# Loading sample rows into idle grid columns, a state update in two rounds, and an output projection spread between attention units

## The chip, the cores and the metric

The kernel runs on one NeuronCore of a Trainium2 chip. The metric is the device time of one execution in microseconds (us); lower is better.

## The reference

One inference step of a streaming encoder with two layers, for 256 frames of a prompt (two blocks of 128 tokens) and 8 streams of 16 frames (a third block, the "sample" block): D = 1024, all in fp32.

```python
for l in range(DEPTH):                        # DEPTH = 2
    xn = rmsnorm(h, norm_mix[l])
    if l == 0: mix = mamba_mixer(xn, ...)     # in-projection, conv of width 4, SSD scan in 8 groups, gate, out-projection
    else:      mix = attention(xn, shared K/V of the stream) @ w_o + b_o   # window 128, sinks, 16 heads, 4 KV heads
    h = h + mix
    h = h + peer(rmsnorm(h, norm_ffn[l]), ...)
y = rmsnorm(h, norm_final)

def peer(xn, w_q, sub_k1, sub_k2, u_tab, v_tab):       # per token: 8 heads, 16 experts of 128*128 each
    q = xn @ w_q;  top 16 of q1 @ sub_k1, of q2 @ sub_k2, then of the 16*16 sums -> eid (128 per token), gate = softmax
    act = gelu(sum_d u_tab[eid] * xn)
    return sum_k (gate * act) * v_tab[eid]
```

## The kernel before

**Layout and precision.** A weight tile of 128x1024 comes as `raw` over SP's queue, ScalarE casts it to `hi` (line 108) and VectorE subtracts to get `lo` (line 109); a product is three matmuls (`hi*hi`, `hi*lo`, `lo*hi`, lines 144 to 146 for `gemm_cols`, line 157 for `gemm_rows`). Matmul results go to one pool of eight PSUM banks (`bank`). The order of each engine's instructions is fixed ahead of the run by a planner that goes through the program with its own estimates of durations; instructions in `pin(...)` keep their program order, the others it may move.

**Scan (`mamba`).** Eight groups of four heads. Each group has conv tiles `b_tile`, `c_tile` and two `x_tile`s (24 matmuls of 384 columns each), then `decay` (line 455: 12 VectorE operations on `ab`, rows fetched over SP), `states`, `outputs`, `turn` (transposes of `y`, line 529) and `carry` (line 542: the new states of the sample streams, eight small matmuls into four banks, added to `s0` by four VectorE operations, line 545), and `store`. A group's later steps run within the next group's tiles; group 1 has an order of its own. The last group's run inside the out-projection of 16 tiles (`out_terms`), whose accumulators hold six banks.

**PEER (`peer`).** The prompt blocks are done densely: `u_step(e2)` for e2 = 0 to 127 multiplies the prompt by a tile of `u` and writes gelu into the grid `G` (`G[0]`: columns 0 to 63, `G[1]`: 64 to 127; a column e of a half is 128x256). In the second half `w_step` multiplies one-hot gate weights into `G[0]` (VectorE's `og`, `oa`, line 1176), and `v_step(e2)` for 128 more steps multiplies the grid by `v`. So a layer has 256 steps s: 0 to 63, 64 to 127 (second half), 128 to 255 (value stage).
The sample block is done by gathering. Its 128 tokens are in four groups of 32, and the block's 128 experts' rows of `u` are gathered in 32 steps per group over POOL's queue (line 1094) into `gath` (three buffers). VectorE multiplies each gathered tile by the group's rows `xg` and sums (line 1132, `u_item`). `xg` is 128x1024, loaded by `load_group` from `xrow` in DRAM over POOL's queue (line 918); it has one buffer, so group g+1 is loaded when item 31 of group g is done. `tick(s)` says how many items are due at step s (`U_DUE`): 30 by step 64, 72 by 128, 110 by 192, 128 by 216. At every 32nd item it pauses for two steps. Rows of `v` for the sample tokens are gathered into idle columns of the grid (`fetch_v`), 24 of them into columns 48 to 63 of `G[1]` before those are written, the rest into `G[0]` when the value stage has read its first columns, and `v_quad` multiplies them.

**Attention.** Sixteen units in the order p p p p s s s s p p p p s s s s (p: a prompt block and a KV head, two banks of scores; s: two sample streams and two KV heads, one bank). In iteration i a unit's mask and scores are made, the transposes of unit i-2 and the values of unit i-3 (`masks`, `transposes`, `scores`, `values`, all pinned). The results are collected in `oT`. Behind the last unit comes the output projection: eight tiles `ct`, three blocks, 144 matmuls of 512 columns in six accumulator banks. Then the norm of `peer(1)`: sums of squares on ScalarE, `rstd` on POOL, `xn` on VectorE (line 896, into `qTp`), transposes (line 905), splits, and the query projection (lines 144 to 146).

Of the kernel before, what the change touches and what calls it, by code (L numbers as in the profile page):

```python
# [9 lines left out]
F32 = mybir.dt.float32  # L10
# [51 lines left out]
def encoder_step(ctx: ExitStack, tc: tile.TileContext, t_in, t_out):  # L62
# [160 lines left out]
    def mamba(h_src):  # L223
        with ExitStack() as c:
# [68 lines left out]
            if True:  # L293
# [103 lines left out]
                class Group:  # L397
# [133 lines left out]

                    def carry(self):

                        s0 = self.s0
                        dve.tensor_tensor(s0.rearrange("p s (r d) -> p s r d", d=64),
                                          s0.rearrange("p s (r d) -> p s r d", d=64),
                                          decS[:, :, self.hs].unsqueeze(3).to_broadcast([P, NSEQ, 4, 64]), op=OP.mult)
                        pss = [bank([P, 2, 256]) for _ in range(4)]
                        for w in range(2):
                            for q in range(4):  # L540
                                rows = slice(32 * q, 32 * q + 32)
                                pin(pe.matmul(pss[q][:, w], self.Bt[rows, 2 + w], self.xde[rows, 2],
                                              start=True, stop=True, tile_position=(32 * q, 0)))
                        for k in range(4):
                            dve.tensor_tensor(s0[:, 2 * k:2 * k + 2], s0[:, 2 * k:2 * k + 2], pss[k], op=OP.add)

# [5 lines left out]
                for g in range(GROUPS):  # L552
                    G_ = Group(g)
                    gs.append(G_)
                    if g == 2:
                        for nm in ("k", "v"):
                            pin(pool.dma_start(t_out["sm_" + nm][:, 0:P - TS, :], t_in["cache_" + nm][:, TS:P, :]))
                    prev = gs[g - 1] if g else None
                    G_.b_tile()
                    if g > 1:  # L560
                        G_.fetch()
                        prev.states()
                        prev.outputs()
                    G_.c_tile()
                    if g == 1:
                        prev.decay()
                        G_.fetch()
                    if g == 0:
                        st_ = steps()
                        next(st_)  # L570
                    if g > 1:
                        prev.turn()
                    G_.x_tile(0)
                    if g == 1:
                        prev.states()
                        prev.outputs()
                        prev.turn()
                    if g:
                        prev.carry()
                    G_.x_tile(1)  # L580
                    if g == 0:
                        G_.gate()
                        next(st_, None)
                        G_.fetch()
                    else:
                        G_.decay()
                        G_.gate()
                        prev.store()
                    G_.tokens()
# [4 lines left out]
                def out_terms():  # L594
                    for ct in range(16):
                        if ct == 2:
                            last.states()
                            last.outputs()
                        elif ct == 5:
                            last.turn()  # L600
                        elif ct == 7:
                            last.carry()
                        elif ct == 9:
                            last.store()
                            sync.dma_start(t_out["convs"], cst)
                        yield (load_split(t_in["w_out"][ct * P:(ct + 1) * P, :]),
                               lambda b, ct=ct: yhi[:, ct, b * P:(b + 1) * P],
                               lambda b, ct=ct: ylo[:, ct, b * P:(b + 1) * P]), 15 - ct
# [14 lines left out]
    def attention():  # L623
        with ExitStack() as c:
# [158 lines left out]
            def transposes(u):  # L783
                PT[u] = []
                for q, sm in enumerate(P_.pop(u)):
                    nkb = sm.shape[2] // P
                    pt = bank([P, 2, nkb, P])
                    for j in range(2):
# [3 lines left out]
                        "p (n k q) -> p n k q", k=nkb, q=P)  # L792
                    if q:
                        dve.tensor_copy(pT, pt)
# [40 lines left out]
            ohi = T(late, [P, 8, NT], F32R, tag="ohi")  # L835
            olo = T(late, [P, 8, NT], F32R, tag="olo")

            def out_terms():
                for ct in range(8):
                    split(ohi[:, ct], olo[:, ct], oT[:, ct])  # L840
                    yield (load_split(t_in["w_o"][ct * P:(ct + 1) * P, :]),
                           lambda b, ct=ct: ohi[:, ct, b * P:(b + 1) * P],
                           lambda b, ct=ct: olo[:, ct, b * P:(b + 1) * P]), 7 - ct

            for i in range(len(todo) + LAG + 1):
                if i in (5, 6, 7):
# [9 lines left out]
                if i in q_at:  # L856
                    q_tile(q_at[i])

            accs = [[bank([P, 512]) for _ in range(2)] for _ in range(NB)]
            gemm_row_loop(accs, out_terms())  # L860
            for b in range(NB):
# [5 lines left out]
    def peer(l):  # L867
        with ExitStack() as c:
# [20 lines left out]
            qTp = T(qpool, [P, 2 * PH, NP], F32, tag="qTp")  # L889
            grow = brow(t_in["ffn_rows"][l], D, qpool, "grow")  # L890
            h = hold["h"]
# [23 lines left out]
            def load_group(g):  # L915
                xg[g] = T(one, [P, D], F32, tag="xg", bufs=1)
                rows = xrow[g]
# [185 lines left out]
            def fetch_v(n, s):  # L1103

                half, e = (1, HE - 16 + 4 * (n % 4)) if s < 2 * HE else (0, 4 * (n % v_bufs(s)))
                assert all(k != (half, e) for k, _ in vrows.values())
# [20 lines left out]
            def u_item(k):  # L1127
# [6 lines left out]
                if j == TG - 1:  # L1134
                    if g + 1 < GR:
                        load_group(g + 1)
                    lay = T(one, [P, GR, TG], F32, tag="cm", bufs=2)
# [81 lines left out]
            done = {"u": 0, "v": 0, "f": 0}  # L1219
            start, paused = [0], {}  # L1220

            def tick(s):
# [6 lines left out]
                want = P if s >= U_DUE[-1][0] else n0 + (n1 - n0) * (s + 1 - s0) // (s1 - s0)  # L1229
                if done["u"] % TG == 0 and done["u"]:  # L1230
                    if s < paused.setdefault(done["u"], s + 2):
                        return
                while done["u"] < want:
# [8 lines left out]
            def quads(s):  # L1242

                while done["v"] < 32 and V_DUE[done["v"]] <= s:
                    v_quad(done["v"])
                    done["v"] += 1
                if s >= 2 * HE - 16 and done["f"] == 4 * V_FIRST and s < 2 * HE + 17:
                    return
# [40 lines left out]
            gpools.append(c.enter_context(tc.tile_pool(name="pg1", bufs=1)))  # L1289
            G[1] = T(gpools[1], [P, HE, NP], F32, tag="G1")  # L1290
            out_s = [bank([P, 512]) for _ in range(2)]
            for e2 in range(HE):
# [11 lines left out]
            for e2 in range(2 * HE):  # L1304
                v_step(e2)
                tick(2 * HE + e2)
                if e2 < HE and e2 % 2 == 1:
# [125 lines left out]
```

## Time and profile before

| | us |
|---|---|
| median of 3 runs | 2586.1 |
| lowest and highest | 2566.3, 2592.02 |
| profiled execution | 2582.15 |
| its span, first to last instruction | 2579.4 |

In the profile PE is TensorE's matmuls, PEld its weight loads (they overlap), DVE VectorE, ACT ScalarE, POOL GpSimd, SP the queue that issues most transfers. Times count from the start of the span. In a timeline row the brackets at the end say how long the engine was idle before the instruction and what ended that. The mean granted clock of TensorE is 0.971 of full speed over the span.

### The profile page before, as it was taken

How to read it: one execution, taken by the hardware profiler on the slowest of the kernel's cores; microseconds unless marked ns; L12 is line 12 of the kernel's file. 1: busy time of each engine (PE TensorE's matmuls, PEld its weight loads, DVE VectorE, ACT ScalarE, POOL GpSimd, SP SyncE). 2: the span in 40 equal slices, each digit the busy share in tenths (PEclk: the TensorE clock that was granted, in tenths of full speed). 3: DMA queues.
4: the chain of work that ended last, by engine and by line, in shares of the span. 5: the costliest groups of instructions: out<-in, count | busy, mean ns of one | idle time of the engine just before them, and what ended most of it. 6: DMA issues, size and time to landing. Idle time of an engine off the chain costs nothing.

```text
span 2579.4 us, 44478 instructions
## 1 busy us (share of the span) xinstructions
PE 2438.5 (95%) x16656; PEld 2046.8 (79%) x16656; DVE 1874.9 (73%) x4151; ACT 1242.6 (48%) x2410; POOL 702.1 (27%) x755
## 2 busy tenths in 40 slices
PE   8899998999989999998999998999989989999998
PEld 7899978999978876666666878999989876656676
DVE  5888736979867797677655645979878788678655
ACT  5555524433546555454344544433456655545343
POOL 2222200022333124346431100012333224346431
PEclk9999998999989999999999979999999999999999
DMA  5445434477879889889996414467789888989995
GB/s 191 171 170 191 155 110 150 149 246 257 287 267 319 254 274 344 299 336 372 362 340 192 131 34 149 139 223 261 281 276 325 268 270 324 322 328 363 371 333 210
DMA packets 179193, 647.67 MB, mean 251 GB/s; under 512 B 23761, under 2 KB 25665, under 8 KB 176321
## 3 DMA queue, kind: packets, MB, share of 16 engines
q1 hardware_dynamic: 99360, 363.76, 40.7%
q0 software_dynamic: 79616, 281.08, 30.9%
q8 instruction: 130, 2.13, 0.3%
q14 instruction: 87, 0.70, 0.1%
HBM read 628.52 MB, written 18.06 MB: 251 GB/s over the span
## 4 chain that ended last, share of the span: by engine, by line
PE 74%; DVE 12%; DMA 8%; issue 2%; ACT 2%; another core or an unknown queue 1%; POOL 0%; SPq 0%; POOLq 0%; DVEq 0%; ACTq 0%
PE bank L157 25%; PE bank L146 10%; PE bank L144 10%; PE bank L145 10%; PE bank L1151 4%; DVE lo L109 3%; PE bank L1160 3%; PE bank L1207 3%; DMA xg<-xrow 2%; DVE gath L1132 2%; PE bank L1193 2%; DMA gath<-in_p_u,eidU 1%; DMA raw<-in_u_t 1%; ACT hi L108 1%; DVE lox L109 1%
## 5 line engine op out<-in xcount | busy, mean ns | idle before, releaser
L108 ACT CAST hi<-raw 128x1024 fp32r<-128x1024 f32 (+1 forms) x475 | 493.6, 1040 | 594.0 <-PE bank L145 362.3
L109 DVE TENSOR_TENSOR lo<-raw,hi 128x1024 fp32r<-128x1024 f32 (+1 forms) x475 | 575.4, 1213 | 214.2 <-ACT hi L108 207.4
L1094 POOL DMA_INDIRECT gath<-in_p_u,eidU x256 | 310.0, 1211 | 948.5 <-DVE gath L1132 515.8
L146 PE MATMUL bank<-xhi,lo 128*128 128x256 f32 (+1 forms) x1344 | 409.9, 306 | 22.8 <-DVE lo L109 22.6
L144 PE MATMUL bank<-xhi,hi 128*128 128x256 f32 (+1 forms) x1344 | 409.1, 305 | 1.2 <-ACT hi L108 1.2
L145 PE MATMUL bank<-xlo,hi 128*128 128x256 f32 (+1 forms) x1344 | 402.3, 299 | 0.0
L1094 POOL DMA_INDIRECT G<-in_p_v,eidT x256 | 281.4, 1099 | 310.3 <-PE bank L1151 231.1
L1132 DVE SCALAR_TENSOR_TENSOR gath<-gath,xg 128x1024 f32<-128x1024 f32 x256 | 310.8, 1217 | 69.9 <-DMA gath<-in_p_u,eidU 40.6
L146 PEld LDWEIGHTS bank<-xhi,lo 128*128 128x128 f32 x1344 | 259.6, 193 | 31.4 <-DVE lo L109 26.9
L144 PEld LDWEIGHTS bank<-xhi,hi 128*128 128x128 f32 x1344 | 260.1, 194 | 12.4 <-ACT hi L108 6.3
L108 ACT CAST phi<-G 128x256 fp32r<-128x256 f32 x232 | 93.2, 404 | 366.5 <-PE bank L157 310.1
L145 PEld LDWEIGHTS bank<-xlo,hi 128*128 128x128 f32 x1344 | 259.9, 193 | 0.3
L144 PE MATMUL bank<-qhi,hi 128*128 128x256 f32 (+1 forms) x792 | 245.4, 310 | 9.8 <-ACT xf L907 8.2
L146 PE MATMUL bank<-qhi,lo 128*128 128x256 f32 (+1 forms) x792 | 239.6, 303 | 2.2 <-DVE lo L109 2.2
L145 PE MATMUL bank<-qlo,hi 128*128 128x256 f32 (+1 forms) x792 | 239.8, 303 | 0.0
L157 PE MATMUL bank<-hi,phi 128*128 128x512 f32 x640 | 202.6, 411 | 13.2 <-ACT phi L108 8.3
L157 PE MATMUL bank<-lo,phi 128*128 128x512 f32 x640 | 204.4, 399 | 7.2 <-DVE lo L109 6.9
L1186 ACT ACTIVATE oa<-ioh,e2T 128x128 f16<-128x128 f16 x512 | 163.1, 390 | 83.7 <-PE bank L1193 61.7
L109 DVE TENSOR_TENSOR plo<-G,phi 128x256 fp32r<-128x256 f32 x232 | 97.5, 422 | 144.7 <-PE bank L157 139.3
L157 PE MATMUL bank<-hi,plo 128*128 128x512 f32 x640 | 201.6, 397 | 0.0
L157 PEld LDWEIGHTS bank<-hi,phi 128*128 128x128 f32 x640 | 117.9, 190 | 69.6 <-ACT hi L108 17.5
L144 PEld LDWEIGHTS bank<-qhi,hi 128*128 128x128 f32 x792 | 152.4, 192 | 11.3 <-ACT xf L907 8.7
(358 smaller groups left out, 4764.7 us busy)
## 6 DMA issues: line engine op xcount, KB each, us to landing
raw<-in_u_t SPq DMA_DIRECT2D x256, 512.0 KB
raw<-in_p_v SPq DMA_DIRECT2D x256, 512.0 KB
raw<-in_w_in SPq DMA_DIRECT2D x32, 512.0 KB
raw<-in_p_w_q SPq DMA_DIRECT2D x32, 512.0 KB
raw<-in_w_z SPq DMA_DIRECT2D x16, 512.0 KB
s<-in_state_ssm SPq DMA_DIRECT2D x8, 1024.0 KB
out_sm_ssm<-s SPq DMA_DIRECT2D x8, 1024.0 KB
raw<-in_w_out SPq DMA_DIRECT2D x16, 512.0 KB
```

The source lines that it names most:

```text
L108: act.copy(hi, raw)
L109: dve.tensor_tensor(lo, raw, hi32, op=OP.subtract)
L144: pe.matmul(ps, whi[:, s], xhi[:, k, c0:c1], start=(k == 0), stop=False)
L145: pe.matmul(ps, whi[:, s], xlo[:, k, c0:c1], start=False, stop=False)
L146: pe.matmul(ps, wlo[:, s], xhi[:, k, c0:c1], start=False, stop=(k == KD - 1))
L157: mm = pe.matmul(ps, x, w[:, hf * n:(hf + 1) * n], start=s_, stop=e_)
L1094: pool.indirect_dma_start(out=tile_, out_offset=None, in_=tab, in_offset=bass.IndirectOffsetOnAxis(ap=idx, axis=0))
L1132: pin(dve.scalar_tensor_tensor(tile_, tile_, 1.0, xg[g], op0=OP.mult, op1=OP.mult, accum_out=au[g][:, j:j + 1]))
L1151: pin(pe.matmul(out_s[hf][32 * q:32 * q + 32, :], cm[:, q], rows[q][:, hf * 512:hf * 512 + 512], start=(r == 0), stop=(r == 31), tile_posi ...
L1160: pe.matmul(ps, raw[:, k * P:(k + 1) * P], xf[:, k], start=(k == 0), stop=(k == KD - 1))
L1186: act.activation(a[:, i], ioh, AF.Square, scale=-1.0, bias=e2T[:, t, 0:1])
L1207: pe.matmul(accs[b][hf], G[e2 // HE][:, e2 % HE, b * P:(b + 1) * P], raw[:, hf * 512:hf * 512 + 512], start=False, stop=False)
```

## The change

In `peer`, odd groups of sample rows get places of their own: group 1 in columns 60 to 63 of `G[1]`, loaded when that half is allocated; group 3 in columns 32 to 35 of `G[0]`, loaded after step 35 of the value stage. Groups 0 and 2 keep `xg`; group 2 is loaded when group 0 ends. The pause goes. The gathered `v` rows of the second half move from columns 48 to 63 to 44 to 59, and the row `grow` of norm weights is put into columns 60 to 63 of `G[0]`.

In the scan, the last group's `carry` runs in two rounds of two banks. In group 1 the previous group's `decay` comes after `x_tile(0)`, its `carry` after `x_tile(1)`, and its `turn` after the group's own `decay`.

In attention, tiles 0 to 3 of the output projection are done for the two prompt blocks between the last four units (four accumulators); the sample block's part of these tiles comes after the units, with the four tiles of `w_o` loaded and split a second time, and then tiles 4 to 7. The copies of the sample units' transposes go to VectorE.

```diff
-                    def carry(self):
+                    def carry(self, n=4):
...
-                        pss = [bank([P, 2, 256]) for _ in range(4)]
-                        for w in range(2):
-                            for q in range(4):
-                                rows = slice(32 * q, 32 * q + 32)
-                                pin(pe.matmul(pss[q][:, w], self.Bt[rows, 2 + w], self.xde[rows, 2],
-                                              start=True, stop=True, tile_position=(32 * q, 0)))
-                        for k in range(4):
-                            dve.tensor_tensor(s0[:, 2 * k:2 * k + 2], s0[:, 2 * k:2 * k + 2], pss[k], op=OP.add)
+                        for q0 in range(0, 4, n):
+                            pss = {q: bank([P, 2, 256]) for q in range(q0, q0 + n)}
+                            for w in range(2):
+                                for q in pss:
+                                    rows = slice(32 * q, 32 * q + 32)
+                                    pin(pe.matmul(pss[q][:, w], self.Bt[rows, 2 + w], self.xde[rows, 2],
+                                                  start=True, stop=True, tile_position=(32 * q, 0)))
+                            for q in pss:
+                                dve.tensor_tensor(s0[:, 2 * q:2 * q + 2], s0[:, 2 * q:2 * q + 2], pss[q], op=OP.add)
...
                     G_.c_tile()
                     if g == 1:
-                        prev.decay()
                         G_.fetch()
...
                     G_.x_tile(0)
                     if g == 1:
+                        prev.decay()
                         prev.states()
                         prev.outputs()
-                        prev.turn()
-                    if g:
+                    if g > 1:
                         prev.carry()
                     G_.x_tile(1)
...
+                        if g == 1:
+                            prev.carry()
                         G_.decay()
+                        if g == 1:
+                            prev.turn()
                         G_.gate()
...
-                            last.carry()
+                            last.carry(2)
...
-                    if q:
+                    if q or u[0] == "s":
                         dve.tensor_copy(pT, pt)
...
+            first = len(todo) - 4
             for i in range(len(todo) + LAG + 1):
...
-            accs = [[bank([P, 512]) for _ in range(2)] for _ in range(NB)]
-            gemm_row_loop(accs, out_terms())
+                if i == first - 1:
+                    accs += [[bank([P, 512]) for _ in range(2)] for _ in range(2)]
+                if 0 <= i - first < 4:
+                    ct = i - first
+                    out_split(ct)
+                    gemm_rows(accs, [out_term(ct)], ct == 0, False)
+
+            accs.append([bank([P, 512]) for _ in range(2)])
+            for ct in range(4, 8):
+                out_split(ct)
+
+            shift = lambda term: (term[0], lambda b: term[1](b + 2), lambda b: term[2](b + 2))
+            for ct in range(4):
+                gemm_rows(accs[2:], [shift(out_term(ct))], ct == 0, False)
+            gemm_rows(accs, [out_term(4)], False, False)
+            gemm_rows(accs, [out_term(5)], False, False)
+            gemm_rows(accs, [out_term(6), out_term(7)], False, True)
...
-            grow = brow(t_in["ffn_rows"][l], D, qpool, "grow")
+
+            grow = G[0][:, HE - 4:].rearrange("p e t -> p (e t)")
+            src = t_in["ffn_rows"][l]
+            sync.dma_start(grow, bass.AP(tensor=src.tensor, offset=src.offset, ap=[[0, P], [1, D]]))
...
             def load_group(g):
-                xg[g] = T(one, [P, D], F32, tag="xg", bufs=1)
+
+                if g % 2:
+                    xg[g] = (G[1][:, HE - 4:] if g == 1 else G[0][:, 32:36]).rearrange("p e t -> p (e t)")
+                else:
+                    xg[g] = T(one, [P, D], F32, tag="xg", bufs=1)
...
-                half, e = (1, HE - 16 + 4 * (n % 4)) if s < 2 * HE else (0, 4 * (n % v_bufs(s)))
+                half, e = (1, HE - 20 + 4 * (n % 4)) if s < 2 * HE else (0, 4 * (n % v_bufs(s)))
...
                 if j == TG - 1:
-                    if g + 1 < GR:
-                        load_group(g + 1)
+                    if g == 0:
+                        load_group(2)
...
-                if done["u"] % TG == 0 and done["u"]:
-                    if s < paused.setdefault(done["u"], s + 2):
-                        return
...
             G[1] = T(gpools[1], [P, HE, NP], F32, tag="G1")
+            load_group(1)
...
                 v_step(e2)
+                if e2 == 35:
+                    load_group(3)
```

## Rows read from the trace of the kernel before

**Rows 1.** The page's engine table: busy us (share of the span) xinstructions.
```profile
PE 2438.5 (95%) x16656; PEld 2046.8 (79%) x16656; DVE 1874.9 (73%) x4151; ACT 1242.6 (48%) x2410; POOL 702.1 (27%) x755
```

**Rows 2.** Waits of the whole span: waiting engine and line <- releaser: us, times, longest.
```profile
DVE gath L1132 <- DMA gath<-in_p_u,eidU: 40.6, 11, 8.6
...
DVE gath L1132 <- DMA xg<-xrow: 29.2, 4, 7.6
```

**Rows 3.** Timeline of VectorE at first items of groups 1 and 3: start, us, instruction.
```profile
715.91 1.23 DVE L1132 SCALAR_TENSOR_TENSOR gath<-gath,xg 128x1024 f32<-128x1024 f32 x1 [7.59 <-DMA xg<-xrow]
...
1089.11 1.23 DVE L1132 SCALAR_TENSOR_TENSOR gath<-gath,xg 128x1024 f32<-128x1024 f32 x1 [8.64 <-DMA gath<-in_p_u,eidU]
```

**Rows 4.** Timeline of TensorE behind the first of these waits.
```profile
719.81 0.58 PE L146 MATMUL bank<-xhi,lo 128*128 128x256 f32 x1 [6.64 <-DVE lo L109]
```

**Rows 5.** Windows: stretch, us, PE PEld DVE ACT POOL busy (xinstructions), PEclk, DMA share, GB/s.
```profile
705.00:755.00 50.00, 40.70 (x346) 38.18 (x344) 31.25 (x50) 22.41 (x47) 12.13 (x11) 0.83 0.75 242
755.00:882.00 127.00, 122.56 (x1199) 112.73 (x1198) 100.22 (x154) 78.26 (x159) 39.33 (x39) 0.99 0.88 301
882.00:923.00 41.00, 35.67 (x331) 34.81 (x330) 30.53 (x48) 23.17 (x48) 8.15 (x8) 0.92 0.79 238
1877.00:1923.00 46.00, 38.40 (x355) 35.56 (x355) 31.57 (x51) 22.64 (x47) 12.15 (x11) 0.89 0.81 264
2050.00:2090.00 40.00, 34.50 (x326) 33.64 (x325) 29.92 (x48) 22.60 (x48) 8.16 (x8) 0.91 0.79 236
```

**Rows 6.** Timeline of POOL: the first gather into the second half's grid.
```profile
689.59 1.01 POOL L1094 DMA_INDIRECT G<-in_p_v,eidT  x1 [1.70 <-ACT xlo L1275]
```

**Rows 7.** Chain that ended last, in time, around boundaries 1, 2 and 3: start, us, what.
```profile
699.80 16.08 DMA xg<-xrow
...
887.49 14.40 DMA xg<-xrow
...
1068.75 0.47 POOL xg L918
...
1069.79 19.20 DMA gath<-in_p_u,eidU
```

**Rows 8.** Timeline, all engines, at the end of the scan and of attention.
```profile
390.95 0.50 PE L157 MATMUL bank<-hi,ylo 128*128 128x512 f32 x1
...
397.31 2.08 DVE L896 TENSOR_SCALAR qTp<-h,rstd 128x1024 f32<-128x1024 f32 x3 [2.18 <-DMA out_sm_ssm<-s]
...
406.16 0.69 PE L144 MATMUL bank<-qhi,hi 128*128 128x384 f32 x1 [3.62 <-ACT xf L907]
...
1566.62 0.63 PE L157 MATMUL bank<-hi,olo 128*128 128x512 f32 x2
...
1577.25 0.69 PE L144 MATMUL bank<-qhi,hi 128*128 128x384 f32 x1 [4.58 <-ACT xf L907]
```

**Rows 9.** Timelines of TensorE and VectorE in the scan's second group.
```profile
64.69 0.45 PE L146 MATMUL bank<-xhi,lo 128*128 128x384 f32 x1 [2.98 <-DVE lo L109]
...
79.52 3.24 DVE L455 SCALAR_TENSOR_TENSOR ab<-ab,acum,msk 128x128 f32<-128x128 f32 x12 [0.33 <-DMA ab<-acum_rows]
...
83.42 1.12 PE L529 MATMUL bank<-ident,y 128*128 128x128 f32 x4 [7.96 <-DVE y L520]
```

**Rows 10.** Windows of attention's last units and projection, and a row of TensorE's timeline.
```profile
1501.00:1510.00 9.00, 5.19 (x52) 3.92 (x48) 6.87 (x23) 5.22 (x20) 0.00 (x0) 0.85 0.01 2
1510.00:1531.00 21.00, 21.00 (x220) 17.36 (x219) 6.55 (x22) 7.09 (x27) 0.00 (x0) 0.50 0.00 1
1531.00:1567.30 36.30, 35.72 (x144) 27.97 (x144) 12.77 (x19) 11.08 (x20) 1.08 (x2) 0.95 0.28 87
...
1508.22 1.94 PE L790 MATMUL bank<-ident,sm 128*128 128x128 f32 x8 [3.81 <-DVE sm L780]
```

**Rows 11.** Groups by line: the weight split (page), copies on VectorE (1501 to 1531).
```profile
L109 DVE TENSOR_TENSOR lo<-raw,hi 128x1024 fp32r<-128x1024 f32 (+1 forms) x475 | 575.4, 1213 | 214.2 <-ACT hi L108 207.4
...
L794 DVE COPY pT<-bank 128x512 f32<-128x512 f32 x1 | 0.7, 692 | 0.4 <-PE bank L790 0.4
```

More of the change, by code (lines that the diff above doesn't have):

```diff
@@ L836, in attention, with out_split, out_term @@
             olo = T(late, [P, 8, NT], F32R, tag="olo")
[L838 to L843, printed above, removed]
+            accs = []
+            def out_split(ct):
+                split(ohi[:, ct], olo[:, ct], oT[:, ct])
+            def out_term(ct):
+                return (load_split(t_in["w_o"][ct * P:(ct + 1) * P, :]),
+                        lambda b: ohi[:, ct, b * P:(b + 1) * P], lambda b: olo[:, ct, b * P:(b + 1) * P])
+            first = len(todo) - 4
             for i in range(len(todo) + LAG + 1):
@@ L1219, in peer @@
             done = {"u": 0, "v": 0, "f": 0}
-            start, paused = [0], {}
+            start = [0]
             def tick(s):
@@ L1246, in quads @@
                     done["v"] += 1
-                if s >= 2 * HE - 16 and done["f"] == 4 * V_FIRST and s < 2 * HE + 17:
+                if s >= 2 * HE - 20 and done["f"] == 4 * V_FIRST and s < 2 * HE + 17:
                     return
```

## Prediction

> **What bounds the kernel now.** I read the engine table first: TensorE is busy for 95% of the span [rows 1], so time can come back only where TensorE waits, or where it runs at its lower clock after a wait. Next the table of waits, for the waits of VectorE that end with a transfer: 29.2 us in four waits for `xg`, 40.6 us in eleven for a gathered row [rows 2]. VectorE works its instructions in a fixed order, so behind such a wait stand the subtractions `lo` of the weight split and the one-hot factors `og`, which TensorE needs. The timeline shows it once in full: VectorE waits 7.59 us for `xg` [rows 3], and TensorE starts its next matmul 6.64 us late, on `lo` [rows 4]. The other three waits for `xg` are of the same size (29.2 us in four), at the first two boundaries of either layer. The third boundary of each layer is different: there VectorE waits 8.64 us for a gathered row, not for `xg` [rows 3].
>
> What such a place costs is read from windows around it. Undisturbed, TensorE gets through 1199 records in 127 us, 9.44 per us [rows 5]. The stretch of the first boundary holds 346 records, worth 36.7 us, and takes 50: 13.3 us lost, idle time and half clock together (its mean granted clock is 0.83). In the same way 5.9 us at the second boundary, and 8.4 and 5.5 us in the second layer [rows 5]: **33.1 us** for the four places.
>
> Three further places matter: the end of the out-projection of the scan, the second group of the scan, and the end of attention.
>
> **The change part by part.** The profiled execution took 2582.15 us with a span of 2579.4; its median is 2586.1, and three runs lie between 2566 and 2592, so 1% (26 us) is about what a measurement of this kernel can tell from no change. The sum is made against 2582.15.
>
> *Groups of sample rows.* The pause of two steps after every 32 rows goes, group 1 is loaded at the head of the second half, group 2 at the end of group 0, group 3 at step 35 of the value stage. The load itself isn't cheaper: it takes 14.40 to 16.08 us from issue to use [rows 7]. Nor is it alone on its queue. In the third boundary a gather issued 1 us behind the load took 19.20 us [rows 7]. So each boundary has two prices, the wait for the group and the wait of the rows behind it.
>
> The Trainium skill (DMA: Bandwidth & Descriptors, section on the anatomy of one DMA on the software path) fits a transfer as 2.0 us plus its bytes over 436 bytes per ns, an estimate of 3.2 us for these 512 KB. The trace doesn't agree, with 14.40 to 16.08 us. By the rule every load would be there in time and the whole boundary would be saved, which is the first rival below.
>
> Second boundary (group 2): its load is issued at the end of group 0, more than the 127 undisturbed us of [rows 5] before its use, and no load is issued at that time any more. The 5.9 + 5.5 = 11.4 us come back in full. First boundary (group 1): the earliest issue is when the new half grid is free; the first gather into it waited until 689.59 us for the last copy of the query operands [rows 6]. Row 32 is due four steps into the half. A step is 24 records of the GEMM and 8 of a weight step, 32 / 9.44 = 3.4 us, so the group is needed at about 703 and lands between 704.0 and 705.7: a wait of 1 to 3 us, where there were 7.59. A wait of 7.59 made TensorE 6.64 late, so this one costs at most 2. But the load of group 2 follows within 10 us on the same queue, and rows 33 to 35 are gathered behind both. A row is issued when its buffer (of three) is free, two to three rows ahead. The code wants 42 rows in 64 steps of 3.4 us, 5.2 us each, so the lead is 10 to 16 us against 19.20: up to 9 us of wait come back. I take half of the 13.3 + 8.4 = 21.7 us, 10.9. Ends: all of it, or none. Third boundary: the load of group 3 moves ahead of its use by seven steps, and rows behind it wait as before; I take nothing, with up to 8 us (the first wait of [rows 3] at half) to be gained. **22.3 us**, between 0 (if the rows behind two loads wait as long again as the group did, which eats the second boundary's gain) and 41.
>
> With no pause VectorE has the same 128 row products to do in a layer, only evenly; the quads' rows move four columns down in the grid, and `grow` into four of its columns: nothing else is issued or waits for these. If `grow` came late, only the row products of `xrow` would wait, far ahead of row 0. No price.
>
> *Last states of the scan in two rounds.* The projection holds six of the eight banks, so `carry`, which asks for four, ends only behind it. Its store follows, and `xn` (written into `qTp`) starts at 397.31 after waiting for that store's landing [rows 8]. From the end of the last projection matmul (390.95 + 0.50) to the first query matmul (406.16) pass 14.7 us; at the end of attention, with no such store, the same chain of norm, transposes and splits takes from 1566.62 + 0.63 to 1577.25, 10.0 us [rows 8]. With two rounds the carry runs at its place in the projection on the two free banks, the same eight matmuls, so TensorE has the same work. The store lands long before. **4.7 us**; between 0 (the second round is planned behind the projection again) and 6.5.
>
> *Second group.* TensorE waits 2.98 us for a `lo` that stands behind the decay of group 0 on VectorE, and 7.96 us for `y` to turn, which stands behind the decay of a later group [rows 9]. The change puts decay, carry and turn of group 0 later, with a conv tile between. The transfers of the decay rows are not earlier, so VectorE's waits stay and only the cover grows, by the 24 matmuls of a conv tile; and the planner that sets the order may pull the decay forward again. I take half of 10.9 us, **5.5**; between -3 (another 2.98) and 10.9.
>
> *Attention's end.* From 1501 to 1567.3 us: 5.19 us busy in 9 with one idle gap of 3.81 us, 21 us at half clock, then 36.3 us of projection [rows 10]. At full clock and without gaps this is 5.2 + 10.5 + 34.8 = 50.5 us, so at most 15.8 us are to be had; the last 1.9 idle us are the next norm's. A third of the projection's 144 matmuls (48) now stands between the last four units, where TensorE waited for softmax, and should hold the clock up. What it adds: four more loads and splits of `w_o` (1.2 us of VectorE each [rows 11]), beside 13.4 us of VectorE work in the first 30 us [rows 10], so hidden (4.9 us if not); one copy per sample unit moves from ScalarE to VectorE, eight of 0.7 us [rows 11], hidden likewise (5.5 if not). Four of the eight banks are held by the accumulators while the units run. No row of before shows units with four banks; if each of four units waited for a bank as long as the one gap here, 3.81, that is 15 us lost and the gain gone. I take **10 us**, nearer to the upper end because the 21 us at half clock follow that one gap of 3.81 us; ends -5 and 14.
>
> **Sum:** 22.3 + 4.7 + 5.5 + 10 = 42.5 us, 2582.15 - 42.5 = 2539.7, and I say **2540**.
>
> **The rivals.**
> First, the loads are hidden in full, because the lead covers them: 33.1 at the first two boundaries, 8 at the third, 4.7, 6 and 10 elsewhere, some 62 us, 2582.15 - 62 = 2520. The Trainium skill's fit for a transfer (same page and section as above) would make this the likeliest case. For it: the loads of groups 2 and 3 lead their use by far more than 16 us. Against it: the 19.20 us behind a load.
> Second, the wait only changes its name: group 1 and group 2 are loaded one behind the other, the rows behind them hold VectorE as long as `xg` did, and the groups bring nothing; 4.7 + 5.5 + 10 = 20.2 us are left, 2582.15 - 20.2 = 2562. For it: the third boundary of each layer is already such a wait (8.64 us, on a gathered row).
> Third, slower: the pauses let the gather queue empty, and without them the rows come late all along the value stage, where `lo` and `plo` stand behind each on VectorE. Today rows cost 40.6 us in 256, 0.16 us each; at 0.17 us more per row the whole gain is gone. If these waits triple, 81.2 us more, 2582.15 - 42.5 + 81.2 = 2621. Against it: between the boundaries the waits are few, eleven in all.
> Fourth, the change doesn't do what it says: the order of each engine comes from a planner that sees its own estimates, so moved lines may be planned back where they were: 2580.
>
> **How the numbers follow.** The forecast has 0.50, the first rival 0.20, the second 0.17, the third 0.07, the fourth 0.06. Below 2560 (faster by over 1%) lie nearly all of the first two and a third of the second rival: 0.74. Slower by over 1% is the third: 0.07, with a little of the fourth 0.08. The rest, 0.18, is within 1%. The range reaches from somewhat below the first rival (the upper ends of the four terms make 72 us: 2510) to somewhat above the second, 2572.
>
> **What the profile would show.** Right: no wait of VectorE on `xg` over 3 us, none at all at the second boundary; the window of the first boundary at over 8.5 records per us; `carry` inside the projection and the first query matmul some 10 us behind the last projection matmul; the projection's first matmuls ahead of the last `values`, and the granted clock at 1.00 through most of the last units. Wrong: waits for `gath` of 7 us and more behind a load, in place of those on `xg`; a gap before a unit's masks or transposes ended by a bank's release; the turn of group 0 still waiting over 5 us.

## The result, and the profile after

The changed kernel takes 2552.0 us in the median of 11 runs (2539.7 to 2559.1) against 2586.5 for the kernel before in the same session (11 runs): a ratio of 0.9877, 95% interval 0.9851 to 0.9903. Its profiled execution took 2552.02 us with a span of 2550.1, 30.1 us less than that of before. The forecast was 42.5 us less, and 2540 us.

The page's engine table of the changed kernel, against [rows 1]: TensorE's idle time, span less busy, falls from 140.9 us (2579.4 - 2438.5) to 118.9 (2550.1 - 2431.2).

```profile
PE 2431.2 (95%) x16655; PEld 2036.9 (80%) x16656; DVE 1883.9 (74%) x4163; ACT 1243.5 (49%) x2406; POOL 701.3 (27%) x755
```

The table of waits, against [rows 2]: the waits on a group are two instead of four, 11.5 us instead of 29.2, and stand under the name of the grid column `G` that now holds group 1. The waits on gathered rows have not fallen (43.6 against 40.6 us).

```profile
DVE gath L1160 <- DMA gath<-in_p_u,eidU: 43.6, 13, 7.3
...
DVE gath L1160 <- DMA G<-xrow: 11.5, 2, 6.3
```

VectorE's timeline, against [rows 3], at the first boundary of layer 0 and at the third. At the first, where it waited once for 7.59 us, it now waits 5.19 for group 1, then 6.29 for a row (and 1.69 for the next):

```profile
695.55 1.23 DVE L1160 SCALAR_TENSOR_TENSOR gath<-gath,G 128x1024 f32<-128x1024 f32 x1 [5.19 <-DMA G<-xrow]
...
708.76 1.23 DVE L1160 SCALAR_TENSOR_TENSOR gath<-gath,G 128x1024 f32<-128x1024 f32 x1 [6.29 <-DMA gath<-in_p_u,eidU]
...
1061.16 1.23 DVE L1160 SCALAR_TENSOR_TENSOR gath<-gath,xg 128x1024 f32<-128x1024 f32 x1 [6.39 <-DMA gath<-in_p_u,eidU]
```

TensorE's timeline behind these two waits, against [rows 4]: one stop of 6.64 us has become two of 3.3 and 3.4.

```profile
698.05 0.74 PE L1221 MATMUL bank<-og,oa 128*128 128x64 f16 x16 [3.31 <-DVE og L1204]
...
711.57 0.58 PE L146 MATMUL bank<-xhi,lo 128*128 128x256 f32 x1 [3.41 <-DVE lo L109]
```

Windows of the first and second boundary of either layer, against [rows 5] (same columns). The first boundary runs at 368 records in 50 us and 313 in 46, 7.4 and 6.8 per us, a little better in layer 0 than the 6.9 of before and worse in layer 1 than its 7.7. The second has no loss left: 9.6 and 10.0 records per us, clock 1.00.

```profile
679.60:729.60 50.00, 41.59 (x368) 38.75 (x366) 30.12 (x49) 23.10 (x48) 18.50 (x17) 0.90 0.89 275
...
1834.00:1880.00 46.00, 37.09 (x313) 34.46 (x312) 27.95 (x43) 20.56 (x44) 13.43 (x12) 0.85 0.88 255
883.00:924.00 41.00, 39.41 (x393) 38.49 (x392) 36.77 (x59) 28.65 (x60) 7.49 (x8) 1.00 0.82 271
2036.00:2076.00 40.00, 40.00 (x399) 39.06 (x397) 36.29 (x57) 27.42 (x57) 7.49 (x8) 1.00 0.84 272
```

POOL's timeline shows why, against [rows 6]: group 1 is loaded as soon as the new half exists, four gathers of `v` rows and one of a `u` row follow, then group 2's load.

```profile
680.41 0.74 POOL L946 DMA_DIRECT2D G<-xrow  x1 [1.73 <-ACT xlo L1300]
...
688.05 0.93 POOL L1122 DMA_INDIRECT gath<-in_p_u,eidU  x1 [0.30 <-issue]
688.98 0.74 POOL L946 DMA_DIRECT2D xg<-xrow  x1
```

In the chain that ended last, against [rows 7], that `u` row is the longest piece of the boundary. It was issued ahead of group 2's load, not behind it:

```profile
688.05 20.68 DMA gath<-in_p_u,eidU
```

The end of the scan, against [rows 8], in the timeline of all engines: 8.8 us from the last projection matmul's end (388.68 + 0.64) to the first query matmul, where there were 14.7. In the second group, against [rows 9], `y` is waited for 2.15 us instead of 7.96.

```profile
388.68 0.64 PE L157 MATMUL bank<-hi,ylo 128*128 128x512 f32 x2
...
398.10 0.69 PE L144 MATMUL bank<-qhi,hi 128*128 128x384 f32 x1 [3.83 <-ACT xf L931]
...
85.41 1.04 PE L529 MATMUL bank<-ident,y 128*128 128x128 f32 x4 [2.15 <-DVE y L520]
```

Attention's end, against [rows 10]: the first projection matmul stands at 1492.47, ahead of the last values at 1517.72, and the windows over the last units and the rest of the projection have the clock at 1.00 throughout.

```profile
1485.40:1520.00 34.60, 31.80 (x346) 25.33 (x346) 24.34 (x69) 20.01 (x71) 0.00 (x0) 1.00 0.20 63
1520.00:1542.60 22.60, 21.37 (x89) 15.86 (x87) 11.53 (x17) 8.97 (x15) 0.98 (x2) 1.00 0.47 162
...
1492.47 0.73 PE L157 MATMUL bank<-hi,ohi 128*128 128x512 f32 x2
...
1517.72 0.29 PE L825 MATMUL bank<-pT,kv 128*64 128x32 f32 x4
```

### The profile page after: what moved, and what is told of

It reads as the page before. It is cut to its first block, busy times and chain, and to the rows that moved or that the text cites. A ratio compares the mean times of both kernels' runs of the same rounds, so it can differ in the third digit from the quotient of the medians.

```text
span 2550.1 us, 44494 instructions
## 1 busy us (share of the span) xinstructions
PE 2431.2 (95%) x16655; PEld 2036.9 (80%) x16656; DVE 1883.9 (74%) x4163; ACT 1243.5 (49%) x2406; POOL 701.3 (27%) x755
## 4 chain that ended last, share of the span: by engine, by line
PE 75%; DVE 11%; DMA 6%; issue 4%; ACT 2%; POOL 1%; another core or an unknown queue 0%; SPq 0%; POOLq 0%; ACTq 0%; DVEq 0%
PE bank L157 25%; PE bank L146 10%; PE bank L144 10%; PE bank L145 10%; PE bank L1179 4%; DVE lo L109 3%; DMA gath<-in_p_u,eidU 3%; PE bank L1188 3%; PE bank L1235 3%; PE bank L1221 2%; DVE gath L1160 2%; DMA raw<-in_u_t 1%; ACT hi L108 1%; PE bank L504 1%; DMA h<-hd 1%
## 5 line engine op out<-in xcount | busy, mean ns | idle before, releaser
L1160 DVE SCALAR_TENSOR_TENSOR gath<-gath,G 128x1024 f32<-128x1024 f32 x128 | 155.7, 1220 | 32.2 <-DMA gath<-in_p_u,eidU 20.5
L1160 DVE SCALAR_TENSOR_TENSOR gath<-gath,xg 128x1024 f32<-128x1024 f32 x128 | 155.4, 1214 | 23.1 <-DMA gath<-in_p_u,eidU 23.1
```

The source lines that it names most:

```text
L1160: pin(dve.scalar_tensor_tensor(tile_, tile_, 1.0, xg[g], op0=OP.mult, op1=OP.mult, accum_out=au[g][:, j:j + 1]))
```

## Experiments

The experiments ran in three later sessions, in which the kernel before took 2546.4, 2545.4 and 2547.5 us. Every ratio is to the kernel before of the same session, with its 95% interval. Theory: the term for the first boundary was mis-sized, because a load is slow and what is queued behind it is late. Rivals: a part takes back what another brings; the queue, the bytes, the order of the loads or the missing pause is the cause.

**The parts alone.** Each is the kernel before with the hunks of one part of the change.

*groups_alone* (hunks from `grow` on). 

> The kernel before with the groups of sample rows alone (rows of groups 1 and 3 in idle columns of the grid, earlier loads, no pause); scan and attention as before. Theory: of the four places only the second boundary of each layer is won, some 7 us each by the profile of the changed kernel, and the first keeps its loss under other names (a wait of 5 to 6 us for group 1, then one of 6 to 7 us for a row gathered behind two loads): 8 to 14 us faster than before, about 0.996. Rival, that the groups do bring the 22 us of the forecast and that another part takes them back: 20 us faster or more, about 0.991.

Measured: 0.9967 (0.995 to 0.9984), 8 us. The groups bring what the theory says and not 22 us.

*scan_alone* (the hunks of the scan). 

> The kernel before with the two edits in the scan alone (decay, carry and turn of group 0 a conv tile later; the last carry in two rounds of two banks). Theory: 2 to 3 us from the second group and 5 to 6 us between the out-projection and the first query matmul, 8 us together, 0.997. Rival, that the second group's turn is worth the forecast's 5.5 and what follows in the scan gives nothing back: 10 us or more.

Measured: 0.9977 (0.9959 to 0.9995), 6 us, with an interval of 1 to 10.

*attention_alone* (the hunks of attention). 

> The kernel before with the output projection spread between the last units alone. Theory: 11 to 12 us, as the profile of the changed kernel has it, since nothing else touches this stretch: 0.9955. Rival, that a part of it came from the other parts (an earlier start of the units): 6 us or less.

Measured: 0.9992 (0.9974 to 1.001), 2 us, at most 7. The theory fell: its 11 us were not there.

*after_again*, the changed kernel, and *before_again*, the kernel before, each unaltered. 

> The changed kernel itself, unaltered, once more beside the others. The three parts alone gave 0.9967, 0.9977 and 0.9992, a product of 0.9936, where the whole gave 0.9877 on another day. Theory: the parts add up on one chip, and the difference is that of two chips: 0.992 to 0.995. Rival: the parts help each other (less waiting in one place keeps the granted clock up in the next): 0.987 to 0.989 again, as before.

> The kernel before itself, for a profile beside the other kernels of this call. Theory of two chips: its span is 2540 to 2550 and the losses at the boundaries of groups are smaller than in its first profile, which the parts alone are then to be compared with. Rival: the span stays near 2580 and the places read as at first.

Measured: the changed kernel at 0.9903 (0.9889 to 0.9917), 24.7 us, and the kernel before with a span of 2538.5. The whole lies between the two expectations: more than the sum of the parts (16 us, with some 8 of uncertainty), less than the first result. The profiles of before differ between the boundaries too. Windows over the same 1060 matmul records, first profile and then before_again, with TensorE stopping five times, four of them for VectorE (4.3 us in all, up to 1.9 us), in the first and never in the second:

```profile
780.00:893.70 113.70, 109.26 (x1061) 100.82 (x1060) 89.21 (x137) 68.77 (x139) 32.05 (x33) 0.98 0.86 291
```
```profile
773.30:880.00 106.70, 106.70 (x1060) 99.05 (x1060) 89.31 (x137) 68.43 (x139) 32.88 (x33) 1.00 0.87 309
```

So 7 of the 41 us between the two spans lie in this stretch alone, and the session counts for more than most parts. What made the first session slower stays open. What the parts are worth is therefore read from places: the time between fixed landmarks of the program, the same in each profile (a column of the grid is known by its gelu on ScalarE, a column of the value stage by its `phi`). Means over all profiles with and without the edit, loads as one transfer by GpSimd where the groups are concerned:

| place | without | with | gain | forecast |
|---|---|---|---|---|
| start to the states of the scan's last group | 319.8 (5 profiles) | 315.0 (9) | 4.8 | 5.5 |
| from there to the first query matmul | 87.4 (5) | 81.7 (9) | 5.7 | 4.7 |
| first boundary, grid columns 56 to 85, both layers | 218.0 (4) | 222.4 (4) | -4.4 | 10.9 |
| second boundary, columns 116 to 121, both | 47.9 (4) | 34.1 (4) | 13.8 | 11.4 |
| third boundary, value columns 40 to 68, both | 247.6 (4) | 247.3 (4) | 0.3 | 0 |
| attention, first mask to last projection matmul | 121.5 (5) | 114.1 (9) | 7.4 | 10 |

Together 27.6 us, between the 24.7 and the 31.8 (1 - 0.9877 of 2586.5) that the two timings of the whole gave. All but one of the rows are within 3 us of the forecast; the first boundary misses it by 15. Its four profiles on either side spread by 8 to 9 us (214.6 to 223.9 without, 218.3 to 226.0 with), so the loss of 4.4 may be none; a gain of 10.9 it is not.

**The form of the load.** *load_spread*, *load_halves* and *spread_before* change the one transfer of `load_group` and nothing else (the last in the kernel before). In the cut below, `AP(rows, ...)` is short for the access pattern on `rows`; its list gives step and count of each dimension, the outermost first:

```diff
-pool.dma_start(xg[g], AP(rows, [[0, GR], [D, TG], [1, D]]))
+for q in range(GR):                                      # load_spread, spread_before
+    pool.dma_start(xg[g][q * TG:(q + 1) * TG], AP(rows, [[D, TG], [1, D]]))
+for q in range(0, GR, 2):                                # load_halves
+    pool.dma_start(xg[g][q * TG:(q + 2) * TG], AP(rows, [[0, 2], [D, TG], [1, D]]))
```

> The changed kernel with each load of a group as four transfers of 32 rows (rows outermost), in place of one transfer with the four copies outermost; the same bytes, the same queue, the same places in the order. Theory: the one transfer is slow because its packets go to a few of the 16 DMA engines (some 100 GB/s while it is alone), and the rows behind it wait for it; spread, a load lands in 4 to 8 us, VectorE's waits for group 1 and for the rows behind the loads shrink from 6 us to under 2, and 8 to 16 us come back (2536 to 2544). First rival, that the bytes set the time (512 KB beside the weights): the load takes 14 us and more as before, and the time stays within 3 us of the changed kernel. Second rival, that the waits go but TensorE is held by something else at these places: the waits shrink, the time doesn't.

Measured: 0.9799 (0.9774 to 0.9824), 51 us faster than before and some 26 faster than the changed kernel by the ratios, more than expected. The first boundary falls from 109.3 and 110.8 us in after_again to 98.8 and 102.4, 18.9 of these 26. DMA issues from 670 to 700 us, around the first boundary (tile, operation, count, KB each, median us to landing), after_again and then load_spread:

```profile
G<-xrow POOLq DMA_DIRECT2D x1, 512.0 KB, 14.8
xg<-xrow POOLq DMA_DIRECT2D x1, 512.0 KB, 23.0
gath<-in_p_u,eidU POOLq DMA_INDIRECT x6, 12.0
G<-in_p_v,eidT POOLq DMA_INDIRECT x4, 17.9
```
```profile
G<-xrow POOLq DMA_DIRECT2D x4, 128.0 KB, 6.9
xg<-xrow POOLq DMA_DIRECT2D x4, 128.0 KB, 13.7
gath<-in_p_u,eidU POOLq DMA_INDIRECT x6, 9.6
G<-in_p_v,eidT POOLq DMA_INDIRECT x4, 8.1
```

The same bytes in the same places land in half the time (group 1) and six tenths of it (group 2), and the gathers between them sooner too. Windows over this boundary (the last two numbers are the DMA engines' busy share and GB/s), after_again and then load_spread: with the one transfer the engines move 283 GB/s, with four 353, and TensorE stays at full clock.

```profile
676.00:730.00 54.00, 47.34 (x415) 44.61 (x414) 34.57 (x54) 27.41 (x57) 20.20 (x18) 0.87 0.90 283
```
```profile
676.00:730.00 54.00, 52.53 (x518) 49.65 (x517) 44.09 (x68) 33.84 (x69) 23.70 (x26) 1.00 1.00 353
```

No wait on a group is left, and the waits of VectorE on rows fall from 43.7 us in after_again to this line:

```profile
DVE gath L1161 <- DMA gath<-in_p_u,eidU: 31.8, 12, 4.8
```

> The changed kernel with each load of a group as two transfers of two copies each (the copies outermost, 64 partitions a transfer). Theory, that a transfer is spread over as many DMA engines as its outermost count has (four for four copies, two for two): a load takes 13 us or more from issue to use, the waits stay, and the time is that of the changed kernel within 5 us. Rival, that smaller transfers are what helped: half of the gain of the four transfers or more, some 20 us faster than the changed kernel.

Measured: 0.9913 (0.9897 to 0.9928), the time of the changed kernel (0.9903). VectorE waited 15.9 us for group 1, once in each layer, and the chain that ended last has the second half's landing, 17 us after its issue:

```profile
682.28 17.05 DMA G<-xrow
```

Halving the transfer brings nothing; rows outermost in place of copies is what helps. The packets in the traces show how: at the head of layer 0, where less else moves, the load's 128 packets of 4 KB were under way four at a time for 5.6 of 9.1 us in after_again and never more than six; with the four transfers of load_spread there were up to 18 at a time, and all were done in 3.5 us. The Trainium skill (DMA: Bandwidth & Descriptors, section "Why a DMA increments its semaphore by 16 and not by 1") says that a transfer is spread over the largest number of engines, at most 16, that divides the slowest dimension of both sides. By that rule it is four for four copies, two for two, 16 for 32 rows; the packets and the times of the three forms agree with it, and which engine carried which packet no run here shows.

> The kernel before with nothing but the load of a group as four transfers of 32 rows. Theory, that the boundaries are lost to slow transfers rather than to late ones: the waits for a group shrink to half or less and 15 to 30 us come back without any of the change, 0.988 to 0.994. Rival, that only the early issue lets the load be hidden: the waits for a group stay over 5 us and the time is the same within 5 us.

Measured: 0.9851 (0.9834 to 0.9868), 38 us, more than the whole change brought, with the loads where they had always been. Its waits on a group, against [rows 2]:

```profile
DVE gath L1133 <- DMA xg<-xrow: 2.9, 2, 2.2
```

Its first boundary takes 97.7 and 100.1 us, its second 17.0 in both layers, as with the groups. Where the load is quick, the groups bring nothing at either of these boundaries.

**The queue, the order and the pause.** *load_sync* is the changed kernel with one word changed:

```diff
-                pool.dma_start(xg[g], ...)
+                sync.dma_start(xg[g], ...)
```

> The changed kernel with the loads of a group issued by SyncE in place of GpSimd, the same single transfer with the copies outermost; the order of TensorE's instructions stays the same. Theory, that the load is slow because it runs on four DMA engines, and the rows behind it are late because they need those same engines: the load still takes 13 us or more, VectorE waits 4 us and more for group 1, and the time is within 6 us of the changed kernel. Rival, that GpSimd's queue is what makes it slow and holds the rows behind it: the waits go and 15 us or more come back.

Measured: 0.9973 (0.9954 to 0.9992), some 18 us slower than the changed kernel in after_again, which ran in another session. The wait for group 1 stays (6.77 us), the next row comes 0.26 us late instead of 6.3, and now the weights are late, which stand behind the load on SyncE's queue. TensorE's timeline, the waits of ScalarE on weights (21.1 us in 9 in after_again), a weight tile behind both loads in the chain, and the row's gather with the product that uses it:

```profile
696.57 0.58 PE L144 MATMUL bank<-xhi,hi 128*128 128x256 f32 x1 [6.16 <-ACT hi L108]
...
ACT hi L108 <- DMA raw<-in_u_t: 75.6, 20, 10.4
...
686.31 29.18 DMA raw<-in_u_t
...
682.25 1.41 POOL L1122 DMA_INDIRECT gath<-in_p_u,eidU  x1 [0.30 <-issue]
...
701.30 1.23 DVE L1160 SCALAR_TENSOR_TENSOR gath<-gath,G 128x1024 f32<-128x1024 f32 x1 [0.26 <-DMA gath<-in_p_u,eidU]
```

The queue isn't what makes the load slow. And the row was hardly quicker for having the load on another queue: 19.0 us from issue to landing (682.25 to 701.3), where it took 20.4 in after_again. Its wait is short for the most part because, counted from the load's issue, it was gathered 1.4 us sooner (6.2 against 7.6) and VectorE came to it 3.2 us later (25.0 against 21.8). At the third boundary of layer 0, though, rows behind the load land after 11.2 and 10.8 us (18.9 and 19.0 in after_again). So the load delays what stands behind it on its own queue, and at the first boundary transfers on the other queue as well; the theory was right in that and wrong about the time, and how much is the queue's and how much the engines' isn't separated.

*group2_late*, in which `k == TG + 12` is row 12 of group 1:

```diff
-                if j == TG - 1:
-                    if g == 0:
-                        load_group(2)
+                if k == TG + 12:
+                    load_group(2)
```

> The changed kernel with group 2 loaded 12 rows into group 1, so that it no longer follows group 1's load within 10 us. Theory of the forecast's text (the rows are late because they are gathered behind both loads): the wait for group 1 stays at 5 to 7 us, the wait for a row behind it shrinks from 6 or 7 us to under 3, and 4 to 8 us come back. Rival, that one slow load is enough: the row's wait stays over 4 us and the time within 3 us of the changed kernel.

Measured: 0.9884 (0.9859 to 0.9909), no different from the changed kernel. It didn't do what it says: the planner issued group 2's load almost where it had been, 10.8 us behind that of group 1 (POOL's timeline; 8.6 in the changed kernel), behind one more row. So a load of group 2 at a distance was not tested here. One thing shows all the same: the row that VectorE waits for now stands 3.2 us ahead of group 2's load (issued at 684.85) and still takes 19.6 us.

```profile
677.20 0.74 POOL L946 DMA_DIRECT2D G<-xrow  x1 [1.72 <-ACT xlo L1300]
...
688.02 0.74 POOL L946 DMA_DIRECT2D xg<-xrow  x1
```

*pause_kept*:

```diff
+                if done["u"] % TG == 0 and done["u"]:
+                    if s < paused.setdefault(done["u"], s + 2):
+                        return
```

> The changed kernel with the pause of two steps after every 32 rows put back. Theory, that leaving the pause out is what brought group 1's row products ahead of their load: the wait for group 1 falls under 2 us (two steps are 6.8 us), the row behind it is less late, and 4 to 10 us come back against the changed kernel. Rival, that the pause only shifts the same rows: the time stays within 3 us, or is longer by the rows that are made up for afterwards.

Measured: 0.9922 (0.9897 to 0.9946), not faster than the changed kernel. The wait for group 1 is gone, as expected, and the wait for the row has grown from 6.3 to 10.25 us (VectorE's timeline); it ends at 709.1, where without the pause it ended at 708.8 (after) and 708.1 (after_again):

```profile
709.10 1.23 DVE L1160 SCALAR_TENSOR_TENSOR gath<-gath,G 128x1024 f32<-128x1024 f32 x1 [10.25 <-DMA gath<-in_p_u,eidU]
```

So the row that lands behind the load sets the end of this boundary, whoever waits first.

*spread_late* has the four transfers and the edit of group2_late. 

> The changed kernel with each load as four transfers of 32 rows and group 2 loaded 12 rows into group 1. Theory: the four transfers brought most of it; what is left at the first boundary are waits for rows of 1 to 3 us behind group 2's transfers (13 to 16 us to land), so this brings 2 to 6 us beyond the four transfers alone, some 0.978 of before. Rival, that rows between the loads wait for the four gathers of value rows and not for group 2: the same as with the four transfers alone, 0.980.

Measured: 0.9793 (0.9766 to 0.9819), 2492.9 us, the same as load_spread. Since the planner put group 2's load back here too, but for one row (689.6 us, 9 behind the last of group 1's), it is load_spread almost unchanged: both beat the changed kernel by some 1%.

## Why the prediction was right, and where it wasn't

2552 us lies inside the stated range, which at 62 us was wide enough to hold one wrong term: by the places, the scan brought 10.5 us (10.2 forecast), attention 7.4 (10), the groups 9.7 (22.3). Of the forecast's own signs, those of the first boundary came out on the wrong side: a wait of 5.19 us for the group instead of at most 3, 7.4 and 6.8 records per us instead of over 8.5, and a wait for a row of 7.3 us.

**Groups, first boundary: the term that was mis-sized.** 10.9 us were expected (half of 21.7), -4.4 were measured over the two layers. Two steps failed. The first: "the group is needed at about 703 and lands between 704.0 and 705.7". The half began 9.2 us earlier than in the kernel before (the load was issued at 680.41; the first gather into that half at 689.59 before), so both times count from there. The load landed 15.1 us after its issue, as forecast; but VectorE asked for it at 690.36 (695.55 - 5.19), 10.0 us after the issue and not 13.6: I had counted four steps of TensorE into the half, while VectorE, which splits weights ahead of TensorE, passes the same place in the program earlier. The second: the lead of a gathered row, 10 to 16 us against 19.20, was taken to bring back up to 9 us of the wait. The lead was 14.4 us (702.47 - 688.05), as forecast, but the row took 20.68. It stood behind one load and four gathers of `v` rows, ahead of group 2's load (688.05 against 688.98), so the two loads in a row, which I blamed, weren't needed for it. And in the kernel before one wait had covered both prices: the row gathered 1 us behind the load was used without a wait, because VectorE had stood for the group until 715.91 (POOL's and VectorE's timelines of before):

```profile
700.85 0.97 POOL L1094 DMA_INDIRECT gath<-in_p_u,eidU  x1 [0.30 <-issue]
...
719.68 1.22 DVE L1132 SCALAR_TENSOR_TENSOR gath<-gath,xg 128x1024 f32<-128x1024 f32 x1
```

With the load moved ahead of the gathers, one wait became two. pause_kept shows the row alone ending the boundary, load_spread that a quicker load takes most of it away. That was the second rival's mechanism, in one place of the two for which it was named. The size of the loss had been read well: with the four transfers and nothing else (spread_before), the first boundary takes 197.8 us over both layers instead of 218.0 in the mean without, 20.2 against the 21.7 of the forecast.

**Second boundary.** "Come back in full", 11.4 us: 13.8, since nothing is left of the loss. The loss itself was read short: the 9.44 records per us that it was measured against come from a stretch with stops of its own, and 1060 records in 106.7 us are 9.93. **Third boundary.** Nothing was taken and nothing came (0.3): the load moved seven steps ahead, but the row behind it still waits 6.39 us.

**Scan.** 4.7 and 5.5 us were expected, 5.7 and 4.8 measured over 14 profiles. The carry ran at its place, 8.8 us from projection to query; `y` waits 2.15 us. The first pair of profiles alone has 2.6 for the second group.

**Attention.** 10 us expected; 10.8 in the first pair of profiles (124.7 to 113.9), 7.4 in the means, 2 (at most 7) by the timing of the part alone. By its own profile the part alone has the stretch at 116.4 us, beside 121.1 and 126.6 in groups_alone and scan_alone of the same session; why less of it reaches the whole is open. The mechanism shows: projection between the units, clock at 1.00 from its first to its last matmul in the first profile of after (50.2 us), though not in every profile: 0.94 and 52.8 us in after_again and attention_alone. By [rows 10] the 36.3 us of projection come to 34.5 at a clock of 0.95, not 34.8, and the "1.9 idle us" stand in no row; neither changes the term. What I took for a fixed cost, 21 us at half clock behind a gap [rows 10], isn't one: in before_again the same place looks like this (a window from just before the transposes on), and the whole stretch takes 118.8 us instead of 124.7.

```profile
1485.00:1510.00 25.00, 22.97 (x248) 18.95 (x250) 10.85 (x36) 11.68 (x42) 0.00 (x0) 0.73 0.01 2
```

Whether the part alone brings 2 or 7 us stays open; so does whether the parts help each other, since 24.7 us against their sum of 16 is about the uncertainty of that sum.

**The rivals.** Loads hidden in full: not so. A load in this form took 14.8 us at the boundary and 11.8 at the quieter head of layer 0 (after_again); with rows outermost, each 128 KB landed in 6.9 us at the boundary and 2.6 at the head (load_spread, medians). The fit of the Trainium skill (DMA: Bandwidth & Descriptors, section on the anatomy of one DMA on the software path) gives an estimate of 3.2 us for the 512 KB and 2.3 us for 128 KB: at the head of the layer the transfers with rows outermost come near it, the one with copies outermost takes over three times as long. Rows late all along the value stage: not seen, 43.6 us of waits on rows against 40.6, and with the pause put back they are longer, 75.5 us. Lines planned back: not in the change itself, but in two of the experiments.

## What to carry to other kernels

Before a slow transfer is moved earlier, ask why it is slow: its form cost more here than its place, and four transfers with rows outermost brought more than all the edits of the change. When an engine's request is dated, count in that engine's own order, not in the steps of the engine that it feeds. A stretch at half clock in one profile is a sample; take its price from several.

## What was unexpected of the hardware

A load of 512 KB with its four copies outermost took 14.8 us; at the quieter head of a layer some four of its packets were under way at a time. What was issued behind it on its queue took 16 to 20 us on GpSimd's queue (gathers, after_again) and 17 to 29 on SyncE's (weights, load_sync; the longest stood behind two loads). In load_sync the row on the other queue took 19 us too. As four transfers of 32 rows it landed in 6.9. And the same 1060 matmul records took 113.7 us at a granted clock of 0.98 in one session, with TensorE stopping five times, four of them for VectorE, and 106.7 at 1.00 without a stop in another. Why VectorE was late in the one is open.
